# Experts of a mixture on one core: 128 tokens in three rounded products, the rest as plain float32 in quarters of the array

## The chip, the cores and the metric

One core of one Trainium2 chip runs the whole kernel. The metric is the device time of one execution in microseconds (us). The engines' names are those of the profile: PE is TensorE's matmul, PEld its weight load, DVE VectorE, ACT ScalarE, POOL GpSimd, SP SyncE, whose queue issues the weight transfers.

## The reference

Two layers of a diffusion backbone over 512 latent tokens and 256 context tokens, 1024 channels, all in float32. Layer 0 is a recurrent mixer and a dense feed-forward part, layer 1 an attention mixer and a mixture of eight experts, of which every token takes two. Only the mixture is concerned here:

```python
def run(args):                      # one block of 128 tokens of one expert
    tok, w, e = args
    xb = xt[tok]
    hid = jax.nn.silu(xb @ w1[e]) * (xb @ w3[e])     # 1024 -> 3584, twice
    return (hid @ w2[e]) * w[:, None]                # 3584 -> 1024
```

The results are added to the stream of each token. For the drawn inputs (seed 0) the reference's routing gives the eight experts, by falling count, 190, 156, 154, 143, 122, 96, 88 and 75 tokens. Each expert's three matrices have 11.0 million float32 values, 44 MB; all eight together 352 MB.

## The kernel before

Layers and stages run one after another; the mixture (`moe`) is the last stage before the final norm. The experts are ranked by count, and rank r has a fixed number of places, `CAPS[r]`: 192, 160, 160, 144 and four times 128. Tokens beyond them would go through a loop of blocks of 128 (`For_i` in `moe`). Experts are taken in four pairs, ranks (0, 4), (1, 5), (2, 6), (3, 7).

`gather` picks a pair's tokens with small bf16 products (`pid`, line 1176), and POOL fetches their rows by an indirect transfer (line 1183); `gates` takes the gates by further small products (`pgt`, line 1210); `gathered` transposes the rows to channel-major (`pgx`, line 1224). Both share two PSUM buffers of the tag `tr`. The gather of the next pair is called within the first products of the current one.

Float32 products are made from parts: `split` (lines 166 and 167) has ACT round a block to a high part (type fp32r) and DVE subtract it to get a low part; then three products are summed, high by high, high by low, low by high. Weights come in blocks of at most 2048 values a partition (1 MB, `unit2`, DMA in line 1148) into four buffers, and each half of a block is split into one of five pairs of buffers.

An expert of up to 128 tokens (`hidden`, `outputs`) has its tokens as the stationary operand, and the weights' parts move as 512 columns (lines 1255 to 1257, 1329 to 1331): three products for each k-tile of 128 channels and 512 columns. An expert of more tokens (`hidden_t`, `outputs_t`) has its weights as the stationary operand, and the tokens' parts move (`turned`, lines 1279 to 1282): one product of n columns and one of 2n for each 128 by 128 block of weights. `weave` takes the two experts of a pair by turns. The order on every engine is the planner's, which lays the instructions out by costs and readiness. Hidden units of the first kind are transposed back (line 1270) and split. Results are scaled and added to the stream in DRAM by an indirect transfer of POOL (`scatter`, line 1315); then `final` loads the stream (line 1457), norms it and stores it.

`ada`, in layer 0, already uses plain float32 in quarters: 32 columns of a stationary operand in one of four column strips of the array, 512 or 256 columns of raw weights moving (line 262). The profile records each such product as two instructions, here called its two passes.

Of the kernel before, what the change touches and what calls it, by code (L numbers as in the profile page):

```python
# [21 lines left out]
P = 128  # L22
D = 1024
# [10 lines left out]
CAPS = (192, 160, 160, 144, 128, 128, 128, 128)  # L34
NX = 16

# columns of the constant table
# [27 lines left out]
# parameters with a value for every channel, as columns of 128 channels  # L65
# [19 lines left out]

class Net:
# [26 lines left out]
    def slot(self, whole=False):  # L113
        """Buffers (raw, high part, low part) of the next block of the weight stream, by turns; only the raw one if `whole`"""
# [17 lines left out]
    def load(self, src, a, b):  # L132
        """A weight block [128, a, b] (a*b <= 2048): its high and low parts for the fast float32 products."""
# [9 lines left out]
        # in pieces, so that what others wait for can come between  # L143
# [5 lines left out]
    def mm3(self, ps, terms, segs, first=True, last=True):  # L149
        """ps[:, seg] = sum over terms of (wh + wl)^T (xh + xl), without wl^T xl."""  # L150
# [10 lines left out]
    def stream(self, tag, dt, name):  # L161
        """A [128, 8, tokens] tile for the latent tokens and one for the context tokens"""
# [7 lines left out]
    def start(self):  # L170
# [19 lines left out]
        # conditioning vectors: for every k-tile columns (lat, ctx) and zeros, the stationary operand of a quarter of the array  # L190
# [25 lines left out]
    def load_z(self, ss, t):  # L216
        """A tile of x or ctx over its root mean squares, channel-major"""
# [9 lines left out]
    def turn(self, dst, src, t):  # L227
        """A tile of tokens into its place in a channel-major stream"""
# [9 lines left out]
    def first_norm(self, k):  # L238
        """h of layer 0 from the normalised streams, for the channels of k-tile k"""
# [8 lines left out]
    def ada(self, l, t, m=4, before=None, tags=None):  # L248
        """128 m columns of the modulation of layer l from 128 t, in four sums (k-tile modulo 4), in a quarter of the array each"""
# [24 lines left out]
    def columns(self, l, t, m, sums, nv):  # L274
        """Columns t ... of the modulation from their sums and the bias, and the scales times the gains"""
# [56 lines left out]
    def spread(self, r, n, pool):  # L332
        """Columns of 128 tokens as n columns, on every partition"""
# [10 lines left out]
    def norm(self, l, which, seg, pool, out=None, full=None, between=None, tags=None):  # L344
        """The parts of the modulated norm of the stream, for one segment of tokens, into out (or HH, HL)"""
# [27 lines left out]
    def residual(self, k, ps, gate, segs):  # L373
        """x += gate * ps for the channels of k-tile k"""
# [5 lines left out]
    def softplus_cols(self):  # L380
        """n4 = -4 * softplus(-lam), p4 = 4 * softplus(-lam): [128, 16] columns"""
# [10 lines left out]
        V.tensor_tensor(x, x, lam, op=ALU.min)                       # -|lam|  # L392
# [22 lines left out]
        V.tensor_tensor(q, q, y, op=ALU.mult)                        # log1p(exp(-|lam|))  # L415
# [16 lines left out]
    def rglru(self):  # L432
# [7 lines left out]
        def out_part(i, ks, first, last, ps=None, segs=SEGS):  # L440
            """The products of channels ks for output channels 128 i ..., and after the last the sum into the stream"""
# [18 lines left out]
        with ExitStack() as st:  # L460
            one = self.pool(st, "rg1", 1)
            two = self.pool(st, "rg2", 2)
            YG = one.tile([P, KT - 1, T], F32, name="YG")           # the last block takes the first place
# [11 lines left out]
            def front(c):  # L475
                """both halves of the input product; the convolution and the GELU"""
# [11 lines left out]
                # centred convolution over both streams, with zeros between them  # L488
# [20 lines left out]
            self.turns, self.wn = [self.wst, self.wst, "x"], 0          # the first block has the third place  # L509
# [3 lines left out]
            for c in range(KT):  # L513
# [19 lines left out]
                if c == KT - 2:  # L533
                    # the products of the input are done: the parts for the next one
# [17 lines left out]
                for d in range(2):  # L552
# [8 lines left out]
                    # 1 - a^2 = tanh(-log a) (1 + a^2)  # L561
# [38 lines left out]
    def new_h(self, v):  # L600
        """New parts of the activations of one kind of tokens"""
# [9 lines left out]
    def open_ffn(self):  # L611
        """Room for it, and its first weights"""
# [926 lines left out]
```

## Time and profile before

| | |
|---|---|
| median of 3 runs | 2407.8 us (2404.79 to 2412.82) |
| span of the profiled execution | 2406.2 us |
| mixture's products, first to last | 1176.9 to 2377.5 us, 1200.6 us |
| busy in the span: PE, DVE, ACT | 97%, 72%, 55% |
| mean granted TensorE clock | 0.987 of full speed |
| DMA over the span | 491 MB, 204 GB/s |

No time is given for the profiled execution beside its span; the median stands 1.6 us above that span. The shares are means over stages with different limits; the stretch of the mixture is read by itself, in the rows below.

### The profile page before, as it was taken

How to read it: one execution, taken by the hardware profiler on the slowest of the kernel's cores; microseconds unless marked ns; L12 is line 12 of the kernel's file. 1: busy time of each engine (PE TensorE's matmuls, PEld its weight loads, DVE VectorE, ACT ScalarE, POOL GpSimd, SP SyncE). 2: the span in 40 equal slices, each digit the busy share in tenths (PEclk: the TensorE clock that was granted, in tenths of full speed). 3: DMA queues.
4: the chain of work that ended last, by engine and by line, in shares of the span. 5: the costliest groups of instructions: out<-in, count | busy, mean ns of one | idle time of the engine just before them, and what ended most of it. 6: DMA issues, size and time to landing. Idle time of an engine off the chain costs nothing. (4 is left out here: it accounts for less than half of the span.)

```text
span 2406.2 us, 36858 instructions
## 1 busy us (share of the span) xinstructions
PE 2331.3 (97%) x14371; PEld 2058.3 (86%) x14371; DVE 1733.8 (72%) x2620; ACT 1333.9 (55%) x1882; POOL 43.1 (2%) x37
## 2 busy tenths in 40 slices
PE   7999999999999999999799999999999999999995
PEld 5876788888888888898699999999999999999994
DVE  6678786555554456695888877889778887788874
ACT  5687442111212145774566665776667766677763
POOL 0000000000000000000100000000000000100000
PEclk9999999999999999999899999999999999999997
DMA  9255523243332111101788888999899998999995
GB/s 299 84 166 185 166 72 122 84 144 123 123 123 68 39 62 54 36 1 45 260 293 284 297 274 287 316 301 314 287 304 315 304 309 287 310 323 312 306 311 176
DMA packets 349429, 491.10 MB, mean 204 GB/s; under 512 B 8848, under 2 KB 247696, under 8 KB 349248
## 3 DMA queue, kind: packets, MB, share of 16 engines
q1 hardware_dynamic: 346032, 477.50, 59.5%
q0 software_dynamic: 3216, 11.18, 2.0%
q8 instruction: 114, 1.87, 0.3%
q14 instruction: 67, 0.55, 0.1%
HBM read 477.04 MB, written 11.60 MB: 203 GB/s over the span
## 5 line engine op out<-in xcount | busy, mean ns | idle before, releaser
L167 DVE TENSOR_TENSOR lo<-raw,hi 128x1024 fp32r<-128x1024 f32 (+2 forms) x856 | 929.4, 1106 | 252.7 <-ACT hi L166 247.6
L166 ACT ACTIVATE hi<-raw 128x1024 fp32r<-128x1024 f32 (+2 forms) x856 | 803.7, 963 | 482.2 <-PE hb L1282 225.4
L1282 PE MATMUL hb<-XG,hi 128*128 128x320 f32 (+2 forms) x1568 | 428.8, 348 | 0.0
L1280 PE MATMUL hb<-XG,lo 128*128 128x160 f32 (+2 forms) x1792 | 398.6, 242 | 0.0
L1280 PEld LDWEIGHTS hb<-XG,lo 128*128 128x128 f32 x1792 | 332.0, 190 | 4.4
L1282 PEld LDWEIGHTS hb<-XG,hi 128*128 128x128 f32 x1568 | 295.1, 188 | 0.0
L1282 PE MATMUL hb<-HT,hi 128*128 128x320 f32 (+2 forms) x864 | 231.5, 348 | 0.0
L1280 PE MATMUL hb<-HT,lo 128*128 128x160 f32 (+2 forms) x896 | 211.1, 239 | 0.0
L157 PE MATMUL p<-HL,hi 128*128 128x512 f32 (+1 forms) x704 | 192.7, 340 | 0.0
L159 PE MATMUL p<-HH,lo 128*128 128x512 f32 (+1 forms) x704 | 191.0, 338 | 0.0
L155 PE MATMUL p<-HH,hi 128*128 128x512 f32 (+1 forms) x704 | 190.1, 337 | 0.0
L1255 PE MATMUL hb<-hi,XG 128*128 128x512 f32 x448 | 178.0, 397 | 1.8 <-ACT XG L166 1.8
L1256 PE MATMUL hb<-hi,XG 128*128 128x512 f32 x448 | 177.3, 396 | 0.0
L1257 PE MATMUL hb<-lo,XG 128*128 128x512 f32 x448 | 176.9, 395 | 0.0
L1280 PEld LDWEIGHTS hb<-HT,lo 128*128 128x128 f32 x896 | 169.9, 190 | 2.4
L1282 PEld LDWEIGHTS hb<-HT,hi 128*128 128x128 f32 x864 | 162.2, 188 | 1.6
L646 DVE TENSOR_TENSOR sg<-p,sg 128x768 f32<-128x768 f32 (+2 forms) x26 | 21.7, 834 | 153.1 <-PE p L159 153.1
L159 PEld LDWEIGHTS p<-HH,lo 128*128 128x128 f32 x704 | 112.9, 188 | 16.6
L1287 ACT ACTIVATE t<-hb 128x320 f32<-128x320 f32 (+2 forms) x128 | 56.9, 445 | 126.6 <-PE hb L1282 126.6
L155 PEld LDWEIGHTS p<-HH,hi 128*128 128x128 f32 x704 | 112.0, 188 | 15.6
L157 PEld LDWEIGHTS p<-HL,hi 128*128 128x128 f32 x704 | 112.9, 188 | 14.2
L377 DVE SCALAR_TENSOR_TENSOR xT<-py,acol,xT 128x512 f32<-128x512 f32 (+1 forms) x176 | 101.8, 612 | 24.8 <-PE py L159 23.9
(413 smaller groups left out, 4092.9 us busy)
## 6 DMA issues: line engine op xcount, KB each, us to landing
raw<-in_moe_w_dram SPq DMA_DIRECT2D x280, 1024.0 KB, 5.2
raw<-in_moe_w_dram SPq DMA_DIRECT2D x64, 896.0 KB, 5.2
raw<-in_ffn_w_dram SPq DMA_DIRECT2D x33, 1024.0 KB, 5.2
raw<-in_ada_w_dram SPq DMA_DIRECT2D x24, 1024.0 KB, 5.2
araw<-in_ada_w_dram SPq DMA_DIRECT2D x48, 512.0 KB, 3.6
raw<-in_rg_w_in_dram SPq DMA_DIRECT2D x16, 512.0 KB, 6.0
raw<-in_attn_w_qkv_dram SPq DMA_DIRECT2D x6, 1024.0 KB, 5.2
raw<-in_rg_w_out_dram SPq DMA_DIRECT2D x4, 1024.0 KB, 5.4
```

What stands on the lines that cost most here:

```text
L155: mm(ps[:, s:e], wh, xh[v][:, s - v * L:e - v * L], start=(first and i == 0), stop=False)
L157: mm(ps[:, s:e], wh, xl[v][:, s - v * L:e - v * L], start=False, stop=False)
L159: mm(ps[:, s:e], wl, xh[v][:, s - v * L:e - v * L], start=False, stop=(last and i == n - 1))
L166: self.nc.scalar.activation(hi, src, AF.Copy)
L167: self.nc.vector.tensor_tensor(lo, src, hi.bitcast(F32), op=ALU.subtract)
L377: self.nc.vector.scalar_tensor_tensor(x, ps[:, s:e], gate[:, k, v:v + 1], x, op0=ALU.mult, op1=ALU.add)
L1255: mm(ps, xh[:, kk], hi[:, k], start=(kk == 0), stop=False)
L1256: mm(ps, xl[:, kk], hi[:, k], start=False, stop=False)
L1257: mm(ps, xh[:, kk], lo[:, k], start=False, stop=(kk == 7))
L1280: mm(ps[:, 0:n], wl, x[:, 0:n], start=False, stop=False)
L1282: mm(ps[:, 0:2 * n], wh, x, start=False, stop=last)
L1287: self.nc.scalar.activation(t, ps[:, :, n:2 * n], AF.Copy)
```

## The change

Only the mixture changes. Each expert's tokens are divided: the first 128 (where there are that many places, `fast`) stay the stationary operand of three rounded products; what is left, `G` groups of 32 tokens, is computed as plain float32 from the raw weights, in quarters of the array. The places become 192, 160, 160, 160, 128, 96, 96, 96, so that G is 2, 1, 1, 1, 0, 3, 3, 3, and ranks 5 to 7 have no rounded part at all. The weights-stationary form is gone. TensorE's order is the program's (`manual_schedule`), in steps of two 1 MB blocks of each expert of the pair: first the rounded products, with one waiting small job (`flush(1)`) after each half block, then the float32 products. There are six raw buffers in place of four, four pairs of split buffers in place of five, one `tr` buffer in place of two, and a bank for the float32 sums (`lv`). `late_tables` takes its scratch from the gathered rows' buffers.

```diff
-CAPS = (192, 160, 160, 144, 128, 128, 128, 128)
+CAPS = (192, 160, 160, 160, 128, 96, 96, 96)
...
-        room = self.mo1.tile([P, D], F32, tag="yt", name="room")
+        room = self.mo2.tile([P, D], F32, tag="gx", name="room", bufs=3)
...
+    def unit(self, src, a, b):
+        raw = self.mr.tile([P, 2048], F32, tag="raw", name="raw")[:, :a * b].rearrange("p (a b) -> p a b", a=a)
         self.nc.sync.dma_start(raw, src)
+        return raw
...
+    def fast(self, X, x, k, hi, lo, first, last):
+        mm, ps = self.nc.tensor.matmul, X["ps"]
+        xh, xl = x[:, k, 0:P], x[:, k, P:2 * P]
+        for n in range(hi.shape[1] // 512):
+            ns = slice(512 * n, 512 * n + 512)
+            mm(ps[:, n], xh, hi[:, ns], start=first, stop=False)
+            mm(ps[:, n], xl, hi[:, ns], start=False, stop=False)
+            mm(ps[:, n], xh, lo[:, ns], start=False, stop=last)
+
+    def exact(self, X, x, k, w, first, last):
+        cw = w.shape[1] // 4
+        for g in range(X["G"]):
+            for j in range(4):
+                self.nc.tensor.matmul(X["pn"][32 * j:32 * j + 32, 256 * g:256 * g + cw], x[:, k, 32 * g:32 * g + 32],
+                                      w[:, cw * j:cw * j + cw], start=(first and g % 2 == 0), stop=last, skip_group_check=True)
+
+    def step(self, Xs, x, xn, views, k0, K):
+        raws = [[self.unit(v, v.shape[1], v.shape[2]) for v in vs] for vs in views]
+        for X, rs in zip(Xs, raws):
+            if X["fast"]:
+                k = k0
+                for raw in rs:
+                    for hi, lo in self.halves(raw):
+                        for i in range(hi.shape[1]):
+                            self.fast(X, X[x], k, hi[:, i], lo[:, i], k == 0, k == K - 1)
+                            k += 1
+                        self.flush(1)
+        for X, rs in zip(Xs, raws):
+            if X["G"]:
+                k = k0
+                for raw in rs:
+                    for i in range(raw.shape[1]):
+                        self.exact(X, X[xn], k, raw[:, i], k == 0, k == K - 1)
+                        k += 1
+
+    def hidden(self, Xs, at=None):
...
+        for c in range(0, FE, 1024):
+            m = min(1024, FE - c)
+            kk = 2048 // m
+            for wi, w in enumerate(("w1", "w3")):
+                for X in Xs:
+                    self.sums(X)
+                for k0 in range(0, KT, 2 * kk):
+                    self.step(Xs, "XG", "XN", [[X[w][:, k:k + kk, c:c + m] for k in (k0, k0 + kk)] for X in Xs], k0, KT)
+                    i += 1
+                    if i == 6 and at:
+                        at()
...
+    def turned_n(self, X, sn, g, f, n):
+        pt = self.tr.tile([P, 512], F32, tag="tr", name="pnt")
+        for b in range(n):
+            self.nc.tensor.transpose(pt[:, b * P:(b + 1) * P], sn[:, b * P:(b + 1) * P], self.ident)
...
+    def rows(self, X, t):
+        G, q = X["G"], 1 if X["fast"] else 0
+        m = 32 * G
+        ps = self.psum().rearrange("p a b -> p (a b)")
+        for j in range(4):
+            for g in range(G):
+                self.nc.tensor.matmul(ps[32 * g:32 * g + 32, 256 * j:256 * j + 256], self.ident[:, 32 * j:32 * j + 32],
+                                      t[:, 256 * g:256 * g + 256], start=True, stop=True, skip_group_check=True)
...
     def experts(self, Xs, then=None):
...
+        with self.tc.manual_schedule(engines={mybir.EngineType.PE}):
+            self.hidden(Xs, lambda: nxt.extend(then() if then else []))
...
+            self.outputs(Xs, turn)
+            if not nxt:
+                self.flush()
...
             self.ms = self.pool(st, "ms", 4)
+            self.mr = self.pool(st, "mr", 6)
             self.hb = self.pool(st, "hb", 3, space=PSUM)
-            self.tr = self.pool(st, "tr", 2, space=PSUM)
+            self.lv = self.pool(st, "lv", 1, space=PSUM)
+            self.tr = self.pool(st, "tr", 1, space=PSUM)
```

`hidden` also passes each 1024 columns' hidden units on: SiLU and product by ACT and DVE, then the transposes (`turned` for the first 128 tokens, `turned_n` for the groups) go onto the list of waiting jobs. `outputs` runs seven steps of the same kind over the second matrix; the groups' results are put back into rows of tokens by `rows`, and the first 128 and the groups of an expert are added to the stream by a `scatter` each.

## Rows read from the trace of the kernel before

**Rows 1.** The page, its first line: span and instructions.
```profile
span 2406.2 us, 36858 instructions
```
**Rows 2.** Windows, the four pairs: length; busy time (count) by engine; clock, DMA share, GB/s.
```profile
1176.90:1496.20 319.30, 318.48 (x1944) 294.76 (x1945) 257.50 (x325) 210.18 (x258) 6.59 (x5) 0.99 0.87 290
1496.20:1794.10 297.90, 297.90 (x1942) 274.65 (x1941) 247.62 (x305) 202.45 (x252) 9.66 (x6) 1.00 0.91 304
1794.10:2092.10 298.00, 298.00 (x1942) 274.50 (x1941) 245.75 (x287) 202.44 (x252) 9.90 (x6) 1.00 0.92 305
2092.10:2377.50 285.40, 285.40 (x1893) 263.04 (x1892) 235.96 (x253) 194.90 (x242) 6.50 (x3) 1.00 0.90 300
```
**Rows 3.** Timeline of PE, tokens stationary: start us, us, engine, line, operation; ten products apart.
```profile
2099.65 0.39 PE L1256 MATMUL hb<-hi,XG 128*128 128x512 f32 x1
...
2101.94 0.39 PE L1257 MATMUL hb<-lo,XG 128*128 128x512 f32 x1
```
**Rows 4.** Timeline of PE, weights stationary, rank 3; five pairs of products apart.
```profile
2355.11 0.34 PE L1282 MATMUL hb<-HT,hi 128*128 128x288 f32 x1
...
2356.33 0.34 PE L1282 MATMUL hb<-HT,hi 128*128 128x288 f32 x1
```
**Rows 5.** Timeline of TensorE, float32 in quarters of 512 columns: the weight loads of two passes.
```profile
234.65 0.13 PEld L262 LDWEIGHTS aps<-raw,cs 128*32 128x32 f32 x4 [0.30 <-issue]
...
235.08 0.13 PEld L262 LDWEIGHTS aps<-raw,cs 128*32 128x32 f32 x4 [0.30 <-issue]
```
**Rows 6.** Timeline of PE, eight quarter products of 256 columns between rounded products.
```profile
35.92 0.52 PE L159 MATMUL pg<-HH,lo 128*128 128x512 f32 x2
...
36.37 1.07 PE L262 MATMUL aps<-raw,cs 128*32 128x256 f32 x16
...
37.37 0.62 PE L155 MATMUL px<-HH,hi 128*128 128x512 f32 x2
...
37.83 0.40 PE L157 MATMUL px<-HL,hi 128*128 128x512 f32 x1
```
**Rows 7.** Timeline of PE, four transposes of hidden units and one product after them.
```profile
2282.29 0.60 PE L1270 MATMUL pht<-ct,sg 128*128 128x128 f32 x4
...
2282.95 0.39 PE L1330 MATMUL hb<-hi,HT 128*128 128x512 f32 x1
```
**Rows 8.** Groups by line and shape, 1180 to 2375 us: count | busy us, mean ns | idle before.
```profile
L167 DVE TENSOR_TENSOR lo<-raw,hi 128x1024 fp32r<-128x1024 f32 x559 | 673.1, 1222 | 131.5 <-ACT hi L166 127.8
...
L167 DVE TENSOR_TENSOR HT<-pht,HT 128x512 fp32r<-128x512 f32 x28 | 19.1, 684 | 0.0
...
L166 ACT ACTIVATE HT<-pht 128x512 fp32r<-128x512 f32 x28 | 16.5, 589 | 0.0
```
**Rows 9.** Timeline, gather of the second pair: its second and its last small product.
```profile
1330.45 0.25 PE L1176 MATMUL pid<-tokid,sel 128*32 128x3 bf16 x4
...
1333.73 0.26 PE L1210 MATMUL pgt<-val,sel 128*128 128x3 bf16 x4
```
**Rows 10.** Timeline around the start of the experts.
```profile
1175.34 1.06 ACT L166 ACTIVATE hi<-raw 128x1024 fp32r<-128x1024 f32 x1 [3.07 <-DMA raw<-in_moe_w_dram]
```
**Rows 11.** Timeline after the last products: the last two scatters.
```profile
2379.74 1.55 POOL L1315 DMA_INDIRECT xd<-yt,ids  x1 [8.18 <-DVE yt L1364]
...
2386.82 1.32 POOL L1315 DMA_INDIRECT xd<-yt,ids  x1 [5.53 <-issue]
```
**Rows 12.** Windows (columns as in rows 2), a stretch with many transfers under way.
```profile
2100.00:2120.00 20.00, 20.00 (x136) 18.57 (x135) 17.08 (x18) 14.56 (x21) 2.08 (x1) 1.00 1.05 355
```
**Rows 13.** Lines 262 and 269 by source, 6 to 8.2 us: count, min/median/max ns, first and last start.
```profile
L262 PE MATMUL aps<-raw,cs x16: 607/634/635, 6.5 to 7.8; 128*32 128x256 f32 x16
L262 PEldq EVENT_SEMAPHORE  x1: 51/51/51, 6.4 to 6.4; - x1
...
L269 PEldq EVENT_SEMAPHORE  x1: 51/51/51, 7.0 to 7.0; - x1
```
**Rows 14.** DMA, 1100 to 2406 us: the gathers' issues, count, us to landing.
```profile
gx<-h2d,ids POOLq DMA_INDIRECT x12, 5.7
```

More of the change, by code (lines that the diff above doesn't have):

```diff
@@ L1216, in gathered @@
     def gathered(self, X):
-        n = X["n"]
-        XG = X["XG"] = self.mo1.tile([P, KT, 2 * n], F32R, tag=f"XG{X['slot']}", name="XG")
-        for gx, a, m in X["gxs"]:
-            for k0 in (0, 4):
-                pt = self.tr.tile([P, 512], F32, tag="tr", name="pgx")
-                for k in range(4):
-                    self.nc.tensor.transpose(pt[:, k * m:(k + 1) * m], gx[:m, (k0 + k) * P:(k0 + k + 1) * P], self.ident[:m, :m])
-                pv = pt[:, :4 * m].rearrange("p (k t) -> p k t", k=4)
-                self.split(XG[:, k0:k0 + 4, a:a + m], XG[:, k0:k0 + 4, n + a:n + a + m], pv)
-            yield
@@ L1229, in flush, with turn @@
-    def flush(self):
-        for f in self.pending:
-            f()
-        self.pending = []
+        n, fast = X["n"], X["fast"]
+        G = (n - (P if fast else 0)) // 32
+        X["G"] = G
+        if fast:
+            X["XG"] = self.mo1.tile([P, KT, 2 * P], F32R, tag=f"XG{X['slot']}", name="XG")
+        if G:
+            X["XN"] = self.mo1.tile([P, KT, 32 * G], F32, tag="XN" if fast else f"XG{X['slot']}", name="XN")
+        def turn(gx, m, q, k0):
+            pt = self.tr.tile([P, 512], F32, tag="tr", name="pgx")
+            for k in range(4):
+                self.nc.tensor.transpose(pt[:, k * m:(k + 1) * m], gx[:m, (k0 + k) * P:(k0 + k + 1) * P], self.ident[:m, :m])
+            pv = pt[:, :4 * m].rearrange("p (k t) -> p k t", k=4)
+            if fast and q == 0:
+                self.split(X["XG"][:, k0:k0 + 4, 0:P], X["XG"][:, k0:k0 + 4, P:2 * P], pv)
+            else:
+                self.nc.scalar.activation(X["XN"][:, k0:k0 + 4], pv, AF.Copy)
@@ L1234, in psum, with flush @@
+        for q, (gx, a, m) in enumerate(X["gxs"]):
+            for k0 in (0, 4):
+                self.pending.append(lambda gx=gx, m=m, q=q, k0=k0: turn(gx, m, q, k0))
+    def flush(self, n=99):
+        for _ in range(min(n, len(self.pending))):
+            self.pending.pop(0)()
     def psum(self):
         return self.hb.tile([P, 2, 512], F32, tag="hb", name="hb")
-    def hidden(self, X):
-        X["HT"] = self.mo1.tile([P, FE // P, 2 * P], F32R, tag=f"HT{X['slot']}", name="HT")
-        for ch in range(FE // 512):
-            yield from self.hidden_512(X, ch)
@@ new lines, in gated @@
+    def gated(self, X, wi, c, m):
+        V, S = self.nc.vector, self.nc.scalar
+        if wi == 0:
+            X["sg"] = self.mo1.tile([P, 1024], F32, tag=f"sg{X['slot']}", name="sg")
+        sg = X["sg"]
+        for n in range(m // 512):
+            ns = slice(512 * n, 512 * n + 512)
+            if wi == 0:
+                S.activation(sg[:, ns], X["ps"][:, n], AF.Silu)
+            else:
+                V.tensor_tensor(sg[:, ns], X["ps"][:, n], sg[:, ns], op=ALU.mult)
+                self.pending.append(lambda n=n: self.turned(X, sg[:, 512 * n:512 * n + 512], c // P + 4 * n))
@@ L1270, in transposed @@
             self.nc.tensor.transpose(pt[:, k * P:(k + 1) * P], sg[:, k * P:(k + 1) * P], self.ident)
[L1271 removed]
+        HT = X["HT"][:, f:f + 4]
         self.split(HT[:, :, 0:P], HT[:, :, P:2 * P], pt.rearrange("p (k t) -> p k t", k=4))
[L1274 to L1282 removed]
@@ new lines, in gated_n @@
+    def gated_n(self, X, wi, c, m):
+        V, S = self.nc.vector, self.nc.scalar
+        G, cw = X["G"], m // 4
+        if wi == 0:
+            X["sn"] = self.mo1.tile([P, 3 * 256], F32, tag=f"sn{X['slot']}", name="sn")
+        sn = X["sn"]
+        s, p = (x[:, 0:256 * G].rearrange("p (g c) -> p g c", g=G)[:, :, 0:cw] for x in (sn, X["pn"]))
+        if wi == 0:
+            S.activation(s, p, AF.Silu)
+            return
+        V.tensor_tensor(s, p, s, op=ALU.mult)
+        for g in range(G):
+            self.pending.append(lambda g=g: self.turned_n(X, sn[:, 256 * g:256 * g + cw], g, c // P, cw // P))
@@ L1316, in scatter, with outputs @@
                                           out_offset=bass.IndirectOffsetOnAxis(ap=X["ids"][:m, q, 1:2], axis=0))
-    def outputs(self, X):
-        V, mm = self.nc.vector, self.nc.tensor.matmul
+    def outputs(self, Xs, at=None):
+        V, S = self.nc.vector, self.nc.scalar
         nf = FE // P
-        ys = self.psum()
-        for u in range(nf // 2):
-            for i, (hi, lo) in enumerate(self.unit2(X["w2"][:, 2 * u:2 * u + 2, :], 2, 1024)):
-                f = 2 * u + i
-                th, tl = X["HT"][:, f, 0:P], X["HT"][:, f, P:2 * P]
+        for X in Xs:
+            self.sums(X)
+        for f in range(0, nf, 4):
+            self.step(Xs, "HT", "HN", [[X["w2"][:, u:u + 2, :] for u in (f, f + 2)] for X in Xs], f, nf)
+            if f == 0 and at:
+                at()
+        for X in Xs:
+            if X["G"]:
+                t = self.mo1.tile([P, 3 * 256], F32, tag=f"sn{X['slot']}", name="yn")[:, 0:256 * X["G"]]
+                S.activation(t, X["pn"][:, 0:256 * X["G"]], AF.Copy)
+                self.pending.append(lambda X=X, t=t: self.rows(X, t))
+            if X["fast"]:
+                yt = self.mo2.tile([P, D], F32, tag="gx", name="yt", bufs=3)
@@ L1380, in experts, with turn @@
     def experts(self, Xs, then=None):
         nxt = []
[L1383 to L1392 removed]
+        with self.tc.manual_schedule(engines={mybir.EngineType.PE}):
+            self.hidden(Xs, lambda: nxt.extend(then() if then else []))
+            def turn():
+                for X in nxt:
+                    self.gathered(X)
+            self.outputs(Xs, turn)
+            if not nxt:
+                self.flush()
@@ L1424, in moe @@
             self.late_tables()
-            self.weave([self.gathered(X) for X in Xs])
+            for X in Xs[::-1]:
+                self.gathered(X)
+            self.flush()
             self.fg = self.mo1.tile([P, D], F32, name="fg")
```

169 lines of the change are left out of this document (41 added, 128 removed).

## The prediction

> **What bounds the kernel now.** I read the page's span first [rows 1], then the windows of the four pairs of experts [rows 2]. In all four PE is busy from end to end: 1199.8 of 1200.6 us. DVE is busy 81 to 83%, DMA 87 to 92%. A busy PE need not be an efficient one, so I asked the timeline for the distance from one product to the next. With tokens stationary, ten products of 512 columns take 2.29 us, 0.229 each [rows 3]. With weights stationary, a low-part and a high-part product of rank 3 together take 1.22/5 = 0.244 us [rows 4]. The last pair has 672 of the latter and 504 of the former: 164 + 115 us; 44 transposes at 0.11 us add 5 (four transposes and a product take 0.66 us, less 0.229 [rows 7]). That is 284 of the 285.4 us that the window has. So PE's own stream of instructions, and no wait, sets the time of this stage; what the change is worth is what it does to that stream, less any wait that it puts in.
>
> **The change part by part.**
>
> *Rounded products.* Ranks 0 to 4 have 128 tokens in this form. One expert needs 8 x 7 x 2 x 3 = 336 products for the hidden units and 28 x 2 x 3 = 168 for the outputs: 504 x 0.229 = 115.4 us; five experts 577 us.
>
> *Float32 in quarters.* The groups of 32 are 2 + 1 + 1 + 1 and 3 + 3 + 3 = 14. The nearest row is the modulation of layer 0, the same form with another operand: four strips at once, two passes each. A pass of 512 columns takes 0.43 us [rows 5], so one of 256 takes 0.215 and a set of four products of 256 columns 0.43 us; two sets and the change of form before and after them fill the 1.00 us from 36.37 to 37.37 [rows 6]. A group needs 48 + 28 sets of 256 columns and 16 of 128 (the last 512 hidden units): 76 x 0.43 = 32.7, and 16 times between 0.215, if a pass scales with its columns, and 0.43, if the weight loads hold it up. I take 0.24, as the columns have set every longer pass: 3.8. So 36.5 us a group, 511 us in all (508 to 555).
>
> *Change of form.* The product pair from 35.92 would have ended its slot at 36.27 (512 + 256 columns, about 0.35 us), and the first pair after the quarters takes 0.46, 0.11 too long [rows 6]. So 36.27 to 37.48 is 1.21 us for two sets worth 0.86: 0.35 us lost for each excursion. There are 14 + 7 steps in each of four pairs: 84 x 0.35 = 29 us.
>
> *Transposes.* 5 x 28 for the first 128 tokens and 14 x 7 for the groups: 238 x 0.11 = 26 us. Putting groups back into rows: seven tiles, each four products long (the groups of one tile run side by side), 7 x (4 x 0.43 + 0.35) = 15 us. Gathers of three pairs, transposes and small products: 10 us.
>
> *Sum of the stream:* 577 + 511 + 29 + 26 + 15 + 10 = 1168 us, where 1200.6 stand now: **33 us less**. Pair 0 gains nothing (two rounded experts and two groups: 322 against 319 us); the other pairs come to 282, against 298, 298 and 285.
>
> *Splits.* 672 halves of blocks become 420; at 1.22 us on DVE [rows 8] that is 308 us less on DVE, and similarly on ACT. Neither holds up PE now, so I cost it at nothing; what it buys is slack.
>
> *Waits added.* PE's order is now fixed, so a small job that is not ready stops everything behind it, and there is one transpose buffer.
> (a) Six small products for the next pair's gather follow one another in PE's order, each needing the buffer back from a DVE copy. Before, four such distances took 3.28 us, 0.82 each [rows 9], with other products between them; now PE stands. Three pairs x 6 x 0.82 = 15 us; 8 if DVE is always free, 36 if each copy sits behind a 1.22 us split [rows 8].
> (b) Transposed hidden units need ACT's 0.59 and DVE's 0.68 us to leave the buffer [rows 8]; with two hand-overs about 1.5 us, and the next job comes after one half block, 6 x 0.229 = 1.37 us. With free engines 0.2 us is lost each time; in pair 0, where DVE has 168 halves x 1.22 = 205 of 322 us, about 0.8. Fourteen such jobs in pair 0, and 21 with 6 of the gathers in the others: 14 x 0.8 + 27 x 0.35 = 20 us; 5 to 40.
> (c) At the start the first product waited for the first weights, split from 1175.34 [rows 10]. Scratch now waits for a gathered row's buffer, so g2's eight products may come later, and six blocks are asked for at once instead of four: 3 us, 0 to 8.
> (d) At the end two scatters 7.1 us apart decide [rows 11]. The last pair now has three, but the one of the first 128 tokens can leave before the float32 products are through: 1 us, -2 to 6.
> Together 39 us, 11 to 90.
>
> *DMA.* A block is now held until the float32 products have read it. In pairs 1 to 3 a step lasts about 13.5 us; its four blocks are released 6.6, 7.5, 10.9 and 13.5 us after its start. The chip moved 355 GB/s at a share of 1.05 [rows 12], so about 338 when full: 3.1 us a block, 12.4 a step. Transfers then end at 9.7, 12.8, 15.9 and 19.0, and the first of these last two is wanted at 27. It fits, at 92% use, as now [rows 2]. SP's queue carries nothing new.
>
> **Forecast:** 2406.2 - 33 + 39 = 2412 us of span, 2414 on the scale of the runs (their median lies 1.6 us above the span). The gain in PE's stream is eaten by waits in the fixed order.
>
> **The rivals.**
>
> *Faster: the waits are mostly hidden.* For it: PE waits for nothing today, DVE and ACT lose a third of their splits, and in pairs 1 to 3 all four halves of a step can be split while float32 products run. With waits near their lower bound, 15 us: 2390. It decides where (a) and (b) together stay under 20 us. Against it: four distances of 0.82 us were measured with two buffers and a free order.
>
> *Float32 passes slower in long runs.* The passes of [rows 5] come in bursts of 16 or 32 instructions; here 256 follow one another. 10% on 511 us is 51: 2465.
>
> *Float32 held by the issue of instructions.* The fastest stream of loads and products that goes on for long is 0.122 us for each load with its product [rows 4]. Were that what the sequencer can do, a set of eight passes would take 0.98 us, not 0.43, and the float32 part 650 us more: about 3060. What speaks against it: the sequencer's wait for line 262 ended at 6.45 us, and its wait for line 269, which stands behind 32 instructions of TensorE, came at 7.0 [rows 13]. That is 0.55 us for 16 passes with their loads, 34 ns a pass, where the strips need one each 54 (0.215 / 4). [...]
>
> *DMA becomes the bound.* If blocks held through the float32 part cut the stream to 295 GB/s, a pair's 88.1 MB takes 299 us, against 282 and 9 of waits: three times 7 or 8, 2436. Against it: 305 GB/s were held with four buffers [rows 2].
>
> *It doesn't do what it says.* Rank 5 has exactly 96 tokens in 96 places. Before, 12 gathers ran, as many as the tiles of the fixed places [rows 14]; were one token routed otherwise, the loop would run one more expert of 128 by itself, its 44 MB taking over 130 us at 338 GB/s: about 2550.
>
> **How the numbers follow.** Forecast 0.54, with its own range 2397 to 2440; hidden waits 0.27 (2376 to 2398); slow passes 0.07; issue 0.02; DMA 0.08; overflow 0.02. No change is what 0.3%, 7.2 us, can't tell: 2400.6 to 2415.0. Of the forecast's chance 0.05 lies below that, 0.25 within and 0.24 above. Faster: 0.27 + 0.05 = 0.32; same 0.25; slower 0.24 + 0.07 + 0.02 + 0.08 + 0.02 = 0.43. The sign is open: the two terms are of one size. Eight in ten: 2380 to 2460, the upper end taking in half of the slow passes and most of the DMA case.
>
> **What would show it.** Right: products of 512 columns still 0.229 us apart; passes of 256 columns 0.215 apart deep within a run of float32; about 0.35 us at each change of form; pairs 1 to 3 at 288 to 295 us, pair 0 at 330; PE idle of some 0.5 to 1 us before transposes and before the gather's products, released by DVE; DVE busy below 60% in pairs 1 to 3. Wrong: PE idle under 10 us in a pair with the pair at 282 (faster), raw blocks as PE's releaser (DMA), passes above 0.22 us (slow float32), more than 12 gathers (overflow), or waits at the steps' starts, where a split comes late, which I cost at nothing because the float32 products cover them.

## The result and the profile after

The changed kernel takes 2428.2 us (median of four runs, 2426.72 to 2429.28) against 2409.07 for the kernel before, measured beside it: a ratio of 1.0079 (95% interval 1.0065 to 1.0094), 0.8% slower. The profiled execution took 2428.55 us with this span, 20.5 us longer than [rows 1]:

```profile
span 2426.7 us, 46682 instructions
```

The windows of the start and of the four pairs, with columns as in [rows 2]; the last one runs to the last turn back into rows:

```profile
1181.80:1187.10 5.30, 5.08 (x30) 3.70 (x28) 4.63 (x16) 3.25 (x5) 0.00 (x0) 0.94 0.44 170
1187.10:1518.90 331.80, 322.87 (x2588) 240.19 (x2587) 234.56 (x266) 196.30 (x207) 5.85 (x5) 0.99 0.77 265
1518.90:1812.30 293.40, 284.47 (x3572) 193.14 (x3568) 127.35 (x182) 98.99 (x114) 9.22 (x6) 0.99 0.82 307
1812.30:2112.70 300.40, 290.12 (x3589) 196.57 (x3585) 125.95 (x164) 98.91 (x114) 10.55 (x6) 0.98 0.81 302
2112.70:2400.60 287.90, 283.81 (x3571) 192.11 (x3568) 118.78 (x135) 93.41 (x105) 4.71 (x3) 1.00 0.81 300
```

PE is no longer busy from end to end: 9 us are missing in pair 0, 9 in pair 1, 10 in pair 2, 4 in pair 3, where 1 us in all was missing in [rows 2]. DVE has half its former load in pairs 1 to 3 (127 of 293 us, 43%), and no row of PE's waits below names a split of weights.

**The stream.** One step of pair 1, PE alone (start, busy us, engine, line, operation): the last rounded product, the float32 products of the two experts, the next rounded product.

```profile
1526.34 0.39 PE L1261 MATMUL hb<-lo,XG 128*128 128x512 f32 x1
1526.66 1.93 PE L1268 MATMUL lv<-raw,XN 128*32 128x256 f32 x32
1528.41 5.36 PE L1268 MATMUL hb<-raw,XN 128*32 128x256 f32 x96
1533.70 0.50 PE L1259 MATMUL hb<-hi,XG 128*128 128x512 f32 x1
```

128 passes, 16 sets, take 7.04 us from 1526.66 to 1533.70. The whole step, 24 rounded products at 0.229 and 16 sets at 0.431, lasts 12.70 us, so an excursion into float32 costs 0.31 us beyond its own work. I took the shortest distance of each kind of stretch that the four pairs show (48 rounded products 11.10 us, 128 passes 7.04, four transposes 0.35 and so on) for every stretch of that kind: their sum is 1160 us, once the waits inside the gathers are out of it. What a stretch takes beyond the shortest is a wait.

**The waits.** PE from 1187 to 2401 us: engine, its tile and line, what it waited for; us in total, times, longest.

```profile
PE hb L1268 <- issue: 7.4, 4, 2.5
PE pgx L1227 <- DVE XG L167: 6.3, 3, 2.8
PE pnt L1355 <- DVE HN L1358: 5.8, 8, 1.3
PE pht L1333 <- DVE HT L167: 5.7, 6, 0.9
PE pid L1174 <- DVE idf L1177: 1.5, 6, 0.3
PE pgt L1208 <- DVE idf L1210: 1.5, 6, 0.3
PE hb L1260 <- issue: 1.4, 1, 1.4
PE pnt L1355 <- DVE HT L167: 0.9, 1, 0.9
PE pgt L1208 <- DVE ids L1185: 0.7, 3, 0.2
```

Three things are to be seen. The transposes (pgx, pnt, pht) wait for the one buffer, as forecast. The gathers' small products (pid, pgt) hardly wait: DVE answers in 0.25 us. And the longest row, "issue", has no releaser: the profile shows nothing that PE waited for. It is four pauses inside the float32 products of the last 512 hidden units; a fifth (1.4 us) lies in the rounded products behind one of them. The second such stretch of pair 1, PE alone:

```profile
1705.53 0.39 PE L1261 MATMUL hb<-lo,XG 128*128 128x512 f32 x1
1705.85 1.96 PE L1268 MATMUL lv<-raw,XN 128*32 128x128 f32 x64
1707.62 4.76 PE L1268 MATMUL hb<-raw,XN 128*32 128x128 f32 x167
1713.83 0.95 PE L1268 MATMUL hb<-raw,XN 128*32 128x128 f32 x25 [1.45 <-issue]
```

After 231 of 256 passes PE stands still, in the middle of a block, with no semaphore behind the wait. What does fall on each of the five pauses is a transfer of PE's own instructions, 16 KB at a time (queue q8), which starts 2.4 to 2.6 us before PE goes on. That this queue is PE's is read from its size: over the span of the kernel before, of this one and of run 1 below it moves

```profile
q8 instruction: 114, 1.87, 0.3%
q8 instruction: 158, 2.59, 0.4%
q8 instruction: 225, 3.69, 0.6%
```

which is 65 bytes for each of PE's 28742, 39954 and 56978 products and weight loads. The queue's row (packets, MB, share) in 26 us around this stretch, then in 26 us of ordinary steps:

```profile
q8 instruction: 4, 0.07, 1.0%
```

```profile
q8 instruction: 2, 0.03, 0.5%
```

Passes of 128 columns use up instructions twice as fast as passes of 256: from 1690.95 us 256 of them took 7.13 us, where 128 of the others took 7.04. Ahead of the pauses the transfers start 6.2 to 7.9 us apart, in steps like the one shown above 8 to 12; the one for this pause starts at 1711.44 and ends at 1712.42, and PE goes on 1.4 us later. Why the next packet is not fetched sooner no run shows.

**The clock.** Windows around the worst wait, that of a gathered row at 1735 us (columns as above):

```profile
1735.20:1738.30 3.10, 0.38 (x2) 0.00 (x0) 2.96 (x4) 3.10 (x5) 0.00 (x0) 1.00 0.02 8
1738.80:1742.10 3.30, 3.30 (x32) 1.54 (x36) 1.77 (x2) 0.28 (x1) 0.00 (x0) 0.50 0.25 21
1742.20:1745.00 2.80, 2.80 (x60) 1.60 (x56) 0.00 (x0) 0.00 (x0) 0.00 (x0) 1.00 0.86 353
```

PE stood for 3.1 us; then the granted clock was 0.50 for 3.4 us, and 32 passes went through in the time of 64: the wait is paid 1.7 us more. Five such spells lie in the experts of this kernel: two behind gathers (1281 and 1899 us), two behind turned rows (1739 and 2039), one behind a pause (1998). In the kernel before, only the first products had the low clock, up to 1183.4 us. PE need not be idle throughout before a spell; the first gather, and the products behind it:

```profile
1277.70:1280.40 2.70, 1.44 (x29) 1.41 (x25) 2.23 (x21) 0.60 (x1) 0.99 (x1) 1.00 0.97 360
1281.40:1284.70 3.30, 3.30 (x9) 2.62 (x8) 2.93 (x16) 1.10 (x2) 1.23 (x2) 0.50 1.01 379
```

In the six kernels here whose gathers' products stand as close (this one and those of runs 1, 2, 3, 5 and 6), a spell follows 15 of 18 gathers; in those of runs 4 and 7 to 12, where other products stand between, it follows none.

**The end** is a little shorter: the scatters of the float32 rows leave 4.3 us apart where [rows 11] had 7.1, and from the last product to the end it is 26.1 us against 28.7.

```profile
2397.37 3.62 PE L1394 MATMUL hb<-yn,ct 128*32 128x256 f32 x32
...
2400.85 1.33 POOL L1362 DMA_INDIRECT xd<-yt,ids  x1 [7.06 <-DVE yt L1397]
...
2405.18 1.43 POOL L1362 DMA_INDIRECT xd<-yt,ids  x1 [3.00 <-issue]
```

### The profile page after: what moved, and what is told of

Same layout as the page of the kernel before. It is cut to its first block, busy times and chain, and to the rows that moved or that the text cites. A ratio compares the mean times of both kernels' runs of the same rounds, so it can differ in the third digit from the quotient of the medians.

```text
span 2426.7 us, 46682 instructions
## 1 busy us (share of the span) xinstructions
PE 2313.2 (95%) x19977; PEld 1774.2 (73%) x19977; DVE 1361.9 (56%) x2215; ACT 1016.5 (42%) x1423; POOL 40.6 (2%) x37
## 5 line engine op out<-in xcount | busy, mean ns | idle before, releaser
L167 DVE TENSOR_TENSOR lo<-raw,hi 128x1024 fp32r<-128x1024 f32 (+1 forms) x588 | 620.0, 1082 | 508.9 <-ACT hi L166 467.3
L166 ACT ACTIVATE hi<-raw 128x1024 fp32r<-128x1024 f32 (+1 forms) x588 | 534.2, 943 | 750.3 <-DMA raw<-in_moe_w_dram 328.0
L1268 PE MATMUL hb<-raw,XN 128*32 128x256 f32 (+1 forms) x4608 | 227.2, 353 | 7.4 <-issue 7.4
L1268 PEld LDWEIGHTS hb<-raw,XN 128*32 128x32 f32 x4608 | 144.3, 110 | 82.6 <-issue 8.4
L1259 PEld LDWEIGHTS hb<-hi,XG 128*128 128x128 f32 x560 | 106.5, 190 | 41.0 <-issue 22.3
L1268 PE MATMUL lv<-raw,XN 128*32 128x256 f32 (+1 forms) x2560 | 132.7, 355 | 0.0
L1261 PEld LDWEIGHTS hb<-lo,XG 128*128 128x128 f32 x560 | 106.2, 190 | 25.5 <-issue 2.2
L1260 PEld LDWEIGHTS hb<-hi,XG 128*128 128x128 f32 x560 | 106.4, 190 | 18.1
L1259 PE MATMUL hb<-hi,HT 128*128 128x512 f32 x280 | 115.2, 412 | 0.0
L1268 PE MATMUL hb<-raw,HN 128*32 128x256 f32 x2016 | 112.7, 379 | 0.0
L1268 PEld LDWEIGHTS lv<-raw,XN 128*32 128x32 f32 x2560 | 74.5, 110 | 51.0 <-issue 12.8
L1261 PE MATMUL hb<-lo,HT 128*128 128x512 f32 x280 | 109.4, 391 | 0.0
```

The costliest lines, as they stand in the source:

```text
L166: self.nc.scalar.activation(hi, src, AF.Copy)
L167: self.nc.vector.tensor_tensor(lo, src, hi.bitcast(F32), op=ALU.subtract)
L1259: mm(ps[:, n], xh, hi[:, ns], start=first, stop=False)
L1260: mm(ps[:, n], xl, hi[:, ns], start=False, stop=False)
L1261: mm(ps[:, n], xh, lo[:, ns], start=False, stop=last)
L1268: self.nc.tensor.matmul(X["pn"][32 * j:32 * j + 32, 256 * g:256 * g + cw], x[:, k, 32 * g:32 * g + 32], w[:, cw * j:cw * j + cw], start=(f ...
```

## The experiments

The theory was: the two forms cost what was forecast or less, and the time went into waits that the fixed order and the one transpose buffer put into PE's stream, into pauses of its instructions, and into the clock that falls behind both. The rivals: the float32 form itself is the cost; or the waits are one queue of late work on ACT and DVE, so that what is taken away at one place comes back at the next. Ratios are to the kernel before, each measured beside it; the changed kernel stands at 1.0079. "Unbroken stream" is the first stretch of 24 or more rounded products in a row. Edits are shown shortened; waits, pauses and clock are those of the one execution of each kernel that was profiled.

**1. Same columns, twice the instructions.**

```
-        for j in range(4):  mm(pn[.., 256*g : 256*g+cw], .., w[:, cw*j : cw*j+cw])
+        for c in range(0, cw, 128):
+            for j in range(4):  mm(pn[.., 256*g+c : 256*g+c+128], .., w[:, cw*j+c : cw*j+c+128])
```

> Every float32 product of 256 columns becomes two of 128, so the same columns go through in twice as many instructions. In the changed kernel five pauses of 1.7 to 2.8 us, four of them in the float32 part of the last 512 hidden units and one in the rounded products behind it, have no releaser; each falls on a fetch of 16 KB of TensorE's instructions whose forerunner came only 6 to 7 us before (elsewhere 9 to 15). Theory (the stream of instructions runs dry where 512 of them, 256 passes and 256 weight loads, follow one another in 7.1 us): each of the 57 full steps of pairs 1 to 3 gets such a pause of about 2 us, some with a fall of the clock behind it; 57 x 2 = 114 us more, time 2490 to 2630. Rival (the pauses belong to the last 512 units: a block or a sum that comes late there): passes of 128 columns cost half of 256, only 57 x 0.08 = 5 us more, time 2428 to 2440.

One run, 2508.2 us: 80 us slower. The row without a releaser, over the experts of this kernel:

```profile
PE hb L1269 <- issue: 46.2, 28, 2.8
```

28 pauses where there were 4, all in float32 products, 25 of them in full steps and 27 at pass 203 or later of a step's 256; and twelve spells of the low clock in place of five. The time lies at the low end of what the theory gave, since about half of the steps pause and not all; the rival's 2440 is out. Blocks and sums are as before, so it is the number of instructions in a step that makes the pauses, and not a block or a sum of the last units.

**2. The last 512 units in two turns.**

```
-        rounded(blocks 0, 1); exact(blocks 0, 1)
+        rounded(block 0); exact(block 0); rounded(block 1); exact(block 1)
```

> Only the steps of the last 512 hidden units: rounded products of the first two blocks, their float32 products, then the same for the other two blocks, in place of all rounded and then all float32. No other step changes. Theory (instruction supply): with 128 passes at a time the five pauses, 10 us, go, and a fall of the clock that follows one of them, 1.7 us; six more changes of form in pairs 1 to 3 and two in pair 0 cost 8 x 0.31 = 2.5 us: 9 us less, 2419. Rival (a block or a sum comes late): the pauses stay, 2430.

2429.1 us, 1.007 (1.0054 to 1.0087): nothing gained. But the pauses are gone, all five, as the theory has it; their place is taken by waits for the last units' transposes, 3.3, 2.0 and 3.1 us. The first of them, on ACT, DVE and PE:

```profile
1714.03 0.60 PE L1334 MATMUL pht<-ct,sg 128*128 128x128 f32 x4
...
1716.38 1.06 ACT L166 ACTIVATE hi<-raw 128x1024 fp32r<-128x1024 f32 x1 [6.54 <-DMA raw<-in_moe_w_dram]
1717.34 0.58 ACT L166 ACTIVATE HT<-pht 128x512 fp32r<-128x512 f32 x1
...
1718.61 0.69 DVE L167 TENSOR_TENSOR HT<-pht,HT 128x512 fp32r<-128x512 f32 x1
...
1719.35 0.33 PE L1356 MATMUL pnt<-ct,sn 128*128 128x128 f32 x1 [3.33 <-DVE HT L167]
```

The transposed units were ready by 1714.6. ACT was idle, but in its order the split of a block stands ahead of them, and that block landed at 1716.4. So PE waits for DVE, DVE for ACT, ACT for a DMA: ACT was idle for 6.5 us, and for the last 1.8 of them the transposed units, one job further back, were ready.

**3. A job behind every second half block.**

```
-                        self.flush(1)
+                        self.tick += 1; self.left -= 1
+                        if self.tick % 2 or len(self.pending) > self.left:
+                            self.flush(1)
```

> The pending transposes are taken behind every second half block, as long as the halves left suffice, and not behind every one. Same work, same buffer. Theory (one transpose buffer, next job asked for it after one half block of 1.4 us): the second-of-two waits in pair 0 (6.8 us before hidden units of 128 tokens, 1.8 before the float32 ones, 1.5 before gathered rows) go, and in pairs 1 and 2 those before gathered rows (3.3 and 3.2 us and two falls of the clock worth 1.7 each); those of pairs 1 to 3 before float32 units (4 to 5 us a pair) stay, since their six jobs have only eight halves: 18 us less, 2410. Rival (the jobs wait for ACT and DVE, which have fallen behind with their splits, whenever they come): within 4 us of 2428.

2405.0 us, 0.9975 (0.9964 to 0.9987): 23 us less. In the same rows the waits for transposes fall from 18.7 us to 3.4, while the pauses stay:

```profile
PE hb L1277 <- issue: 8.9, 4, 2.5
PE pnt L1365 <- DVE HN L1368: 2.5, 3, 1.3
...
PE hb L1269 <- issue: 1.3, 1, 1.3
...
PE pht L1343 <- DVE HT L167: 0.9, 1, 0.9
```

Pair 0 takes 323 us in place of 332, pair 2 292 in place of 300. The rival is out: ACT and DVE keep up if they are given 2.8 us in place of 1.4. It is more than forecast because the waits in pairs 1 to 3 before float32 units went as well (4 to 5 us a pair became 1 to 3).

**4. The gathers' small products among the pending jobs.**

```
-            ps = self.tr.tile(...); matmul(ps, sel, tokid); ...
+            def rowids(): ps = self.tr.tile(...); matmul(ps, sel, tokid); ...
+            self.pending.append(rowids)
```

> The six small products of each later pair's gather are put among the pending jobs, one behind each half block, and no longer follow one another. Theory (each stands until DVE has copied the one before, and the thin stretch of 2.7 us drops the clock for 3.4 us twice in three): a gather's 2.7 us become six times 0.25 = 1.5, and two falls of the clock worth 1.6 us go: 3 x 1.2 + 3.2 = 7 us less, 2421; the gathers' clock spells at 1281 and 1899 us are gone from the records. Rival (the products cost what they cost wherever they stand, and DVE's copies behind splits of 1.2 us make each wait longer): no change or up to 5 us more, 2428 to 2433.

2422.9 us, 1.006 (1.0043 to 1.0077): 5 us less, the interval just overlapping that of the changed kernel. The spells behind the gathers are gone, and the experts take 1206.1 us from the unbroken stream to the last product where they took 1213.5. That is the forecast 7, partly lost again before the experts begin, and partly by luck: the gathers account for 3.7 us of waits and two spells, 6.9 us, but the spells at 1739 and 1998 us are absent too (a wait of 2.7 us at 1738.9 has none behind it here), and the waits before the groups' units went up from 5.8 to 8.4.

**5. The scratch in a buffer of its own.**

```
-        room = self.mo2.tile([P, D], F32, tag="gx", name="room", bufs=3)
+        room = self.mo1.tile([P, FE // P, 64], F32, tag="HN", name="room")...
```

> The scratch of late_tables takes the buffer of HN, which nobody wants for another 60 us, and no longer the third of the gathered rows. Theory (the scratch waits until the first gathered rows have left, at 1176.2 us; its tables and g2's products then fall among the first expert products, and the unbroken stream starts at 1187.1 with 2.8 us lost since 1181.8): the scratch is cleared some 12 us earlier, g2's products stand before the transposes, and the stream starts 5 to 8 us earlier: 2421. Rival (the start is set by the turned rows, whose single buffer ACT and DVE empty between splits of the first blocks): the tables come earlier and the stream doesn't, within 2 us of 2428.

2429.1 us, 1.009 (1.0072 to 1.0108). The scratch is cleared at 1148.4 us in place of 1176.7, g2's products come 18 us earlier, and the stream starts at 1185.5 in place of 1187.1, no more than the starts of these kernels differ among themselves (1185.5 to 1191.6). The rival holds.

**6. Ranks 5 to 7 at 128 tokens again.**

```
-CAPS = (192, 160, 160, 160, 128, 96, 96, 96)
+CAPS = (192, 160, 160, 160, 128, 128, 128, 128)
```

> One part undone: ranks 5 to 7 take 128 tokens in rounded products again, as rank 4 does; order, buffers and the groups of 32 stay. Theory (the float32 form pays a little): for each of three pairs 504 products x 0.229 = 115.4 us come for 3 x 76 x 0.431 + 48 x 0.22 = 108.8; seven jobs of transposes (3.4) and their waits in a full row (7 x 1.1 = 7.7, as in pair 0) come for 21 float32 jobs (5.0), their waits (4), the pauses in instruction supply (4) and a longer turn back into rows (1.9): 2 to 4 us a pair, 2434 to 2440 in all; DVE 20% busier there. Rival (whole experts in float32 are what made it slower): 10 us or more faster, 2418 or less.

2445.9 us, 1.0151 (1.0135 to 1.0166): 17 us slower, so whole experts in float32 gain. The time is above the 2434 to 2440 of the theory: the experts take 13.5 us more, just over the 6 to 12 forecast, and the rest lies at the start and at the end. The waits before hidden units go up as reckoned, 18 more of 0.95 us:

```profile
PE pht L1333 <- DVE HT L167: 22.7, 24, 1.0
```

**7. No fixed order.**

```
-        with self.tc.manual_schedule(engines={mybir.EngineType.PE}):
+        with ExitStack():
```

> TensorE's instructions are left to the order that the scheduler finds, as in the kernel before; nothing else changes. Theory (the fixed order lets a job that is not ready stop everything behind it, some 35 us of waits): these waits shrink, but where the scheduler mixes the forms each change costs 0.31 us; with as many changes as now 2400, with twice as many 2426. Rival (the fixed order protects the blocks: mixed forms, and blocks held longer): slower, 2440 to 2500.

2404.9 us, 0.9983 (0.9973 to 0.9992): 23 us less, by one line. In pair 0 the scheduler mostly puts 11 or 12 rounded products between a job of transposed hidden units and the next where the fixed order has 6, and goes into float32 98 times, not 84 (14 x 0.31 = 4.3 us). Its waits before hidden units are gone altogether, its pauses are not. The rival is out.

**8. Five edits at once:** 2, 3, 4, 5, and two float32 groups in one job of transposes.

```
-        for g in range(G): self.pending.append(lambda g=g: self.turned_n(X, sn[...], g, ...))
+        for g in range(G): self.groups.append((X, sn[...], g, ...))
+        # behind both experts
+        for a in range(0, len(self.groups), 2):
+            self.pending.append(lambda gs=self.groups[a:a + 2]: self.turned_n(gs))
```

> Five edits at once: transposes behind every second half, the gathers' small products among them, scratch in HN's buffer, two float32 groups in one job of transposes, and the last 512 units in two turns of rounded and float32. Theory (the waits are separate and add up): from 2405 with spaced jobs, 5 for the gathers, 5 to 8 for the start, 10 for the pauses and their clock less 2.5 for changes of form, 2 for the paired jobs: 2382, 1.1% faster than the kernel before. Rival (one wait covers another: what is taken away at one place comes back at the next, as the pauses did when only the last units were split up): 2395 to 2405.

2388.8 us, 0.9911 (0.9898 to 0.9925): faster than both kernels, 7 us above the sum of the terms. The 5 to 8 put down for the scratch did not come: the stream starts at 1189.1. Its four pairs, with columns as in [rows 2], and below them all waits of PE in them:

```profile
1189.10:1510.30 321.20, 320.20 (x2589) 238.99 (x2587) 231.81 (x261) 195.31 (x207) 6.62 (x4) 1.00 0.80 273
1510.30:1792.80 282.50, 281.58 (x3573) 192.56 (x3569) 127.31 (x182) 98.79 (x114) 8.18 (x6) 1.00 0.86 319
1792.80:2077.30 284.50, 283.61 (x3589) 193.24 (x3585) 126.29 (x165) 98.62 (x114) 8.42 (x6) 1.00 0.86 318
2077.30:2360.60 283.30, 282.14 (x3572) 192.58 (x3568) 118.27 (x135) 93.40 (x105) 4.83 (x3) 1.00 0.83 306
```

```profile
PE pnt L1383 <- DVE HT L167: 3.8, 4, 1.1
PE hb L1280 <- issue: 0.2, 1, 0.2
```

The clock holds 1.00 throughout. 1171.5 us from the unbroken stream to the last product is what the two forms cost when almost nothing waits, against 1200.6 before.

**9. The same, with rank 0's rows turned first.** In the changed kernel the first turned row waits for the last of three gathers, which is issued when the first blocks of weights are under way (a gather takes 8.2 us to land, 5.7 in [rows 14]):

```profile
1163.11 0.95 POOL L1181 DMA_INDIRECT gx<-h2d,ids  x1 [0.31 <-DVE val L1204]
...
1171.79 1.09 PE L1227 MATMUL pgx<-ct,gx 128*128 128x128 f32 x4 [7.64 <-DMA gx<-h2d,ids]
```

```
-            for X in Xs[::-1]:
+            for X in Xs:
                 self.gathered(X)
```

> All five edits, and the rows of rank 0 are turned first at the start, in place of those of rank 4. In the kernel with the five edits the first turned row waits until 1173.8 us for the last of three gathers, issued at 1164.2 behind blocks of weights; the first expert product needs rank 0's rows, whose gather was issued at 1161.6 and which come third through the one transpose buffer; the unbroken stream starts at 1189.1. Theory (the start is a chain of gather, one buffer, splits): rank 0's rows are turned from about 1167 us, before the first blocks are split, and the stream starts 6 to 10 us earlier: 2381. Rival (the start is set by the first blocks and by ACT and DVE, which then have the turned rows of rank 4 to split among rank 0's products): 2 us or less, 2387.

2382.3 us, 0.9893 (0.9876 to 0.9909). The rows are turned from 1167.6 us and the first product comes at 1176.3, as in the kernel before, where the five edits had it at 1183.2; it then waits for a block's split:

```profile
1176.26 0.80 PE L1280 MATMUL hb<-hi,XG 128*128 128x512 f32 x1 [4.41 <-ACT hi L166]
```

The unbroken stream starts 1.9 us earlier with 13 more products behind it (3.0 us): 4.9 us by the trace, 4 by the ratios, whose intervals overlap. So both sides were half right: the order of the rows counts, and the splits take over.

**10. The five edits without the fixed order.**

> All five edits, and TensorE's order left to the scheduler. Dropping the fixed order alone brought 23 us. Theory (it brought them by the waits that the five edits take away too): within 4 us of 2389. Rival (a free order also finds work for what is left, some 14 us of waits before turned rows and at the start): 2378 to 2384.

2389.2 us, 0.9923 (0.9907 to 0.994): no difference. Once the jobs are spaced, a free order brings nothing more.

**11. The five edits, ranks 5 to 7 at 128.**

> All five edits, with ranks 5 to 7 back at 128 tokens in rounded products. Theory (what the whole experts in float32 bring is PE's stream, not waits): a step of four blocks takes 11.10 + 1.86 = 12.96 us (from the run with this part undone alone) and not 12.70, the last two 12.98 and not 13.1: 4.7 us a pair; the transposes 3.4 more for 2.5 + 1.9 less: 4 to 6 us a pair, 12 to 18 in all: 2401 to 2407. Rival (it was waits: without the row of transposes the two forms cost the same): within 4 us of 2389.

2403.4 us, 0.9981 (0.9972 to 0.9991): 0.7% above the five edits, some 17 us, as forecast from the stream alone. The rival is out.

**12. The five edits without the second.**

> The five edits without the one that takes the last 512 hidden units in two turns; alone that edit ended the pauses and gave their 10 us back as waits before the next transposes. Theory (those waits came from jobs that followed one another, which spaced jobs cure): with the others in place its worth shows: without it the pauses return, 10 us and one fall of the clock of 1.7, less 2.5 for changes of form: 9 us slower than the five together, 2396 to 2400. Rival (it is worth nothing here either): 2386 to 2391.

2397.9 us, 0.9951 (0.9938 to 0.9965): 0.4% or 9.6 us slower than the five, as forecast. The pauses are back (8.7 us in rows without a releaser), though the fall of the clock that the sum counted did not come. An edit that was worth nothing alone is worth 9 us once the jobs behind it are spaced.

## Why the prediction was right, and where its terms were not

The direction that had the largest chance came, and the range held the time; the forecast of 2414 was 14 us short. Its mechanism stands: PE's stream got shorter, by 40 us where 33 were forecast, and waits ate it. That the miss is only 14 is in part luck: the pauses and the low clock, 18 us, were not in the sum, (b) and (c) were 15 too small, and against these stand 22 by which the stream, (a) and (d) came out better than forecast. Term by term, in us against the kernel before:

| term | forecast | measured | from |
|---|---|---|---|
| stream of PE | 1168, -33 | 1160, -40 | shortest distances; run 8 bears it out with 1171.5, waits and eight more changes of form in it |
| (a) gathers' products | 15 | 4 | waits on pid and pgt |
| (b) one transpose buffer | 20 | 30 | 8.9 before hidden units, 12.8 before float32 units, 8.0 before rows |
| (c) start | 3 | 8 | unbroken stream at 1187.1, not 1176.9, less 11 products (2.5) before it |
| (d) end | 1 | -3 | 26.1 against 28.7 |
| pauses of instructions | not priced | 10 | five stretches |
| low clock | 0 | 8 | five spells of 1.3 to 1.7 |
| rest | 0 | 4 | distances under 0.5 |
| sum | +6 | +21 | spans 2406.2 and 2426.7 |

- *Stream.* Rounded products at 0.229, sets of 256 columns at 0.431, as [rows 3, 5]. The change of form was 0.31, not 0.35 (84 x 0.04 = 3 us), and a set of 128 columns 0.22, not 0.24 (224 x 0.02 = 4 us): half of 0.431, so these passes scale with their columns. "Pair 0 gains nothing" held (321 in run 8), and the other pairs came to 282 to 284 there.
- *(a)* was sized from [rows 9], distances of 0.82 us between which other products ran. With PE standing, DVE answered in 0.25. The step mistook a distance for a wait. As much again, 3.2 us, came from the two spells of the clock behind the gathers.
- *(b)* named the right wait, and nearly its size in pair 0, 0.95 us by the profile, but six of the fourteen jobs there had it, not all: by the distances, hidden units of the first 128 tokens waited 8.9 us where its count gives 18.6 (14 x 0.8 + 21 x 0.35). It left out the 56 jobs of the groups' units, which waited 12.8, and had 2.1 (6 x 0.35) for gathered rows, which waited 8.0. In these DVE has a split of 1.2 us or a block's late landing ahead of the copy: before 1933.9 us the copy of transposes made at 1930.8 stood behind the split of a block that landed at 1931.0. Runs 3 and 7 show that more distance between jobs cures this with one buffer; a second buffer under the fixed order was not tried.
- *(c)* was put down to the scratch and to six blocks asked for at once. Run 5 clears the scratch of it; run 9 shows the order in which the rows go through the one buffer. What six blocks at once cost was not tried. The kernel before ran its first 6.5 us at a granted clock of 0.50, up to 3 us lost; with these put down to the start and not to the stream, the stream gains 37 and the start costs 5.
- *Splits at nothing* held in so far as PE waited for no split of weights from 1187 us on. But splits that stand ahead in ACT's and DVE's order lengthen the waits of (b), at 1735 us here, and in run 2 they became the wait.
- *Held by issue.* The rival of 3060 was rightly refused by [rows 13]: 16 sets at 0.431 us are 6.9 us for 128 passes and 128 loads, 0.027 us an instruction. (Its price was reckoned too low: 14 x 92 sets at 0.98 us are 1262, some 750 us more, not 650.) But the refusal looked at how fast instructions are issued and never at how fast they are brought. The program runs 27% more instructions (46682 for the 36858 of [rows 1]), and in this kernel the pauses stand only where 512 come in 7.1 us, or just behind. That is the step that failed: a limit was cleared by its rate in a burst of 32 instructions.
- *Clock.* Waits were counted at face value. The windows around 1735 us show 0.50 behind a wait for splits of a block that landed late. But the like wait of run 4, 2.7 us, has no low clock behind it, and at the gather of 1277.7 us PE was busy for 1.44 of 2.70 us and the clock fell behind it all the same.
- *The rivals.* Hidden waits, priced at 2390, is what run 8 made of the kernel by hand: 2388.8. Slow passes in long runs: none, 0.431 a set in runs of 256 instructions. DMA as the bound: no, pairs 1 to 3 moved 300 to 307 GB/s here and 306 to 319 in run 8, where they take 282 to 284 us; a late block entered by ACT's order alone. Overflow: twelve gathers, as [rows 14].

## What to carry to other kernels

A form of product that saves a few per cent of an engine's stream (40 of 1200 us here) is worth what the jobs between its products let through: before fixing an engine's order, space the jobs that share a buffer by their whole evacuation, two engines' queues included, and count 1.3 to 1.7 us more, as in the five spells here, for a wait that the clock may fall behind. Price an instruction stream by its count as well as by its columns: halving the columns of a pass cost nothing here (0.22 us a set against 0.431) until 512 instructions came in 7.1 us, and pauses with them (10 us in all). And an edit that shows nothing alone may be covered by another wait; put it in with the others and take it out there.

## What the runs showed of the hardware that was not expected

- PE stood in five places with no releaser in the profile: 1.7 to 2.8 us a time from one weight load to the next, each on a 16 KB packet of q8, four where 512 instructions are used in some 7 us and one just behind. Doubling the instructions for the same columns brought 28 such pauses and 80 us; with 256 at a time, in run 2, no wait without a releaser was longer than 0.3 us.
- The granted clock was 0.50 not only after waits of some 3 us but behind 2.7 us of thin work (PE busy for 1.44 of 2.70 us), six groups of four products with three columns each, in 15 of 18 cases; spread out, the same products left it alone (runs 4 and 7 to 12).
- Quarter passes of 256 columns keep 0.431 us for eight over runs of 128 passes, with 128 weight loads between them; no loss grew with the length of the run.
